# Output projection with MLP's first products: transposes half a tile later, another order of tile pairs, four of seven operands split in place

## The chip, the cores and the metric

The kernel runs on one core of a Trainium2 chip. The metric is the device time of one execution in microseconds, as the median over runs. Engines are named as in the profile: PE (TensorE; its weight loads are PEld), DVE (VectorE), ACT (ScalarE), POOL (GpSimd) and SP (SyncE, which here only issues DMAs). A DMA that POOL issues goes over its own queue.

## The reference, cut to what matters

One layer of an encoder over 2048 positions and 1024 channels. Attention and a Hyena operator each give 512 channels. The change touches what comes after them:

```
mix = concatenate([rms_norm(att, attn_out_g), rms_norm(hy, hy_out_g)], axis=-1)
h = h + mix @ w_out
m = rms_norm(h, norm2_g)
h = h + square(relu(m @ w_mlp_in)) @ w_mlp_out
return rms_norm(h, final_g)
```

All matrix products are made in three passes of a split format: an operand is written as high part + low part (a cast on ACT, then a subtraction on DVE), and high·high, high·low and low·high are added up in PSUM.

## The kernel before, in words

The positions lie in 16 tiles of 128. The output projection is made in two halves. The first, `att_part`, multiplies the attention channels; it is a generator that is advanced a step at a time (`pump(side)`) inside the long convolutions of `filter_dft` and `conv`, and writes `h` to `h_d`. A step is three matmuls; a tile has 8 steps.

The second half is `mix`. It runs 16 tiles in a hand-written order; on PE, DVE, ACT and POOL instructions stand in the order of the code, while SP's queue is ordered by the planner. For tile number `n` of the loop (its products are called P(n) here):

- `load` fetches `h` (3 buffers) and the two parts of the Hyena channels (3 sets of buffers), two tiles ahead, over SP.
- `products(u, j, ...)`: 2 column halves j of 4 x 3 matmuls each into a bank per half.
- `added(u, j)` (DVE, L843) takes the bank times the norm plus `h` into `h`. `squared` (ACT, L847) sums squares. `normed` (L855 to L864) writes `h` back to DRAM (the profile names this `h_d<-h`), works out the reciprocal root in five small DVE steps and one ACT square root, and writes `m`, half on DVE and half on ACT.
- `turned` (L870), called T(n) here, transposes `m` by 8 PE instructions into a bank pair. `taken` (L884) moves these with the gain by 8 ACT instructions into `sa` (first tile of a pair, 2 buffers) or `sb` (second tile; 1 buffer with places for 5 blocks: two for the tile itself, three for sums).

Two tiles of a pair (rows `i` and `i + 4` of a half, `half` 0 or 1) give seven operands of MLP's Strassen-Winograd product: four blocks of `m` and three sums of them, by four DVE subtractions (L894) that are queued in `sums` and called by `add_up`. `keep` (L891, POOL DMAs) copies each of the seven: for half 0 into the tiles `ml`, for half 1 into DRAM (`mo_d`). For half 0 a cast on ACT (L912, `cast`) writes `mh` from `ml`, and `rest` (L919, DVE) subtracts it to leave the low part in `ml`. In tile `n` of the loop before, P(n) comes first on PE and T(n-1) after it, once tile n-1 has been added, squared and normed.

Behind the last tile the generator `mlp_in` is advanced by `next(mlp)`: it casts MLP's weight operands (`prepare`, L1013 and L1014) and makes its first products g(block, p). Its first five products are written out in `mix`; the rest follow when `mix` is done. The sums of the weights for the second block (`left_sums`, L796 to L799) are POOL's.

Of the kernel before, what the change touches and what calls it, by code (L numbers as in the profile page):

```python
# [23 lines left out]
NT = SEQ // P  # L24
# [13 lines left out]
def f32(ap):  # L38
    return ap.bitcast(F32)
# [727 lines left out]
def att_part(k, pool, ps, ts):  # L767

    nc, x = k.nc, k.a["x"][0]
    ops = []  # L770
    yield from att_operands(k, ps, ts[0], ops)
    for i, t in enumerate(ts):
        nxt = []
        steps = att_operands(k, ps, ts[i + 1], nxt) if i + 1 < len(ts) else iter(())
        for j in range(2):
            at = slice(t * P, (t + 1) * P), slice(j * 512, (j + 1) * 512)
            h = pool.tile([P, 512], F32, name="h", bufs=HB)
            nc.sync.dma_start(out=h[:], in_=x[at])
            for _ in project(k, ps, j, h[:], k.wo0, *ops):
                pump(steps)  # L780
                yield
            nc.sync.dma_start(out=k.h_d[at], in_=h[:])
        ops = nxt
# [26 lines left out]
LAST_USED = 0, 1, 5, 2, 4, 3, 6  # L810


def mix(k, mo, pool, top, ps, wo, mlp):


    nc, a = k.nc, k.a
# [1 line left out]
    nc.scalar.dma_start(out=g2[:], in_=a["norm2_g"][0].rearrange("(d p) -> p d", p=P), allow_slow_non_contiguous=True)  # L818
    made = {(part, i): mo.tile([P, 4, 4, P], F32R, name=f"m{part}{i}", bufs=1) for i in LAST_USED for part in "hl"}
    k.mh, k.ml = ([made[part, i] for i in range(7)] for part in "hl")  # L820
    order = [(half, i, s) for half in range(2) for i in range(4) for s in range(2)]
    tiles = [8 * half + 4 * s + i for half, i, s in order]
    hr, = k.hr

# [26 lines left out]
        u.m = (pool if own else mo).tile([P, DM], F32, name="m", tag="h" if own else "raw", bufs=3 if own else NRAW)  # L851
        u.ssq = pool.tile([P, 1], F32, name="r2s", bufs=2)

    def normed(u):
        nc.sync.dma_start(out=k.h2_d[u.t * P:(u.t + 1) * P, :], in_=u.h[:])  # L855
        y, r, e = (pool.tile([P, 1], F32, name=f"r2{x}", bufs=2) for x in "yre")
        nc.vector.tensor_scalar(out=y[:], in0=u.ssq[:], scalar1=EPS, scalar2=None, op0=ALU.add)
        nc.scalar.activation(out=e[:], in_=y[:], func=AF.Sqrt)
        nc.vector.reciprocal(out=r[:], in_=e[:])
        nc.vector.tensor_mul(out=e[:], in0=r[:], in1=r[:])  # L860
        nc.vector.scalar_tensor_tensor(out=e[:], in0=e[:], scalar=-0.5, in1=y[:], op0=ALU.mult, op1=ALU.mult)
        nc.vector.scalar_tensor_tensor(out=r[:], in0=e[:], scalar=1.5, in1=r[:], op0=ALU.add, op1=ALU.mult)
        nc.vector.tensor_scalar_mul(out=u.m[:, :512], in0=u.h[:, :512], scalar1=r[:])
        nc.scalar.mul(out=u.m[:, 512:], in_=u.h[:, 512:], mul=r[:])  # L864
# [8 lines left out]
    def taken(u):  # L873


        half, i, s = u.order
        if s == 0:
            k.sa = pool.tile([P, 2, 4, P], F32, name="sa", bufs=2)
        else:
            k.sb = top.tile([P, 5, 4, P], F32, name="sb", bufs=1)  # L880
        b = k.sb if s else k.sa
        for c in range(2):
            for d in range(4):
                nc.scalar.mul(out=b[:, c, d], in_=u.tp[:, c, d * P:(d + 1) * P], mul=g2[:, 4 * c + d:4 * c + d + 1])  # L884
        if s:
            op = [k.sa[:, 0], k.sa[:, 1]] + [k.sb[:, j] for j in range(5)]
            b11, b21, b12, b22, t1, t2, t4 = op
            def keep(*js):
                for j in js:
                    dst = k.mo_d[j, :, i] if half else f32(k.ml[j][:, i])  # L890
                    nc.gpsimd.dma_start(out=dst, in_=op[j])  # L891

            def sub(out, in0, in1, *js):
                nc.vector.tensor_sub(out=out, in0=in0, in1=in1)  # L894
                keep(*js)

            keep(0, 1)
            sums.append(lambda: sub(t1, b12, b11, 4))
            sums.append(lambda: sub(t2, b22, t1, 5, 3))
            sums.append(lambda: sub(b12, b22, b12, 2))  # L900
            sums.append(lambda: sub(t4, b21, t2, 6))
            if not half:
                sums.append(lambda: splits.extend((j, i) for j in (0, 1, 5, 3, 4, 2, 6)))

    def add_up(n):
        for _ in range(min(n, len(sums))):
            sums.pop(0)()

    def cast(n):
        for _ in range(min(n, len(splits))):  # L910
            j, i = splits.pop(0)
            nc.scalar.copy(out=k.mh[j][:, i], in_=f32(k.ml[j][:, i]))  # L912
            casts.append((j, i))

    def rest():
        while casts:
            j, i = casts.pop(0)
            hi, lo = k.mh[j][:, i], k.ml[j][:, i]
            nc.vector.tensor_sub(out=lo, in0=f32(lo), in1=f32(hi))  # L919

    sums, splits, casts = [], [], []
    queue = [load(0), load(1)]
    old = older = None
    for n in range(NT):
        u = queue.pop(0)
        if n + 2 < NT:
            queue.append(load(n + 2))
        if n == NT - 2:
            next(mlp)
        if n == 0:  # L930
            v = queue[0]
            for w in (u, v):
                for j in range(2):
                    products(w, j, (0, 1, 2))
            for j in range(2):
                products(u, j, (3,))
        elif n == 1:
            for j in range(2):
                products(u, j, (3,))
        elif n < NT - 1:  # L940
            for j in range(2):
                products(u, j, range(4))
        else:
            for c in range(4):
                for j in range(2):
                    products(u, j, (c,))
        if old:
            added(old, 1)
            squared(old)
            rest()  # L950
            cast(1)
            normed(old)
            if older:
                taken(older)
            turned(old)
        room(u)
        if n < NT - 1:
            added(u, 0)
        if n % 2 == 0 or n == NT - 1:
            add_up(5)  # L960
        cast((2 - n % 2) if n < NT - 1 else 99)
        older, old = old, u
    rest()
    next(mlp)
    for j in range(2):
        added(old, j)
    next(mlp)
    squared(old)
    next(mlp)
    normed(old)  # L970
    next(mlp)
    taken(older)
    turned(old)
    next(mlp)
    taken(old)
    add_up(99)
# [2 lines left out]
LEAD = 5  # L979


def mlp_in(k, mo, ps):
# [78 lines left out]
    early = []  # L1061
    for x in seq[:2]:
        prepare(*x)
        early.append(product(*x))
    lefts(0)
    yield
    for x in seq[2:LEAD]:
        prepare(*x)
        if x is not seq[LEAD - 1]:
            yield  # L1070
    for x in seq[2:LEAD - 1]:
        early.append(product(*x))
    yield
    early.append(product(*seq[LEAD - 1]))
    yield
    held.update((name, tile(name, bufs)) for name, bufs in (("sn", 2), ("u2", 1), ("u4", 1), ("r", 4)))
    for i, (n, p) in enumerate(seq):
        if i + LEAD < len(seq):
# [562 lines left out]
def conv(k, o, c1, ps, side):  # L1641
# [104 lines left out]
    for gb in range(16):  # L1746
        cur = nxt
        if gb < 15:
            nxt = turned(gb + 1)
        if o and gb < 11:  # L1750
            pump(side, 10 ** 6 if gb == 10 else PUMP_C[3])
        both = c1.tile([P, 2, HYW], F32, name="both", tag="F", bufs=FB)
        gx, y = (both[:, i].rearrange("p (g m) -> p g m", m=P) for i in range(2))
        nc.sync.dma_start(out=gx, in_=gate[:, 4 * gb:4 * gb + 4])
        pair = ps.get("x", "yo")
        yo = pair[:, 0].rearrange("p (q g m) -> p q g m", q=2, m=HF)
        for q in range(2):
            for half in range(2):
                nc.tensor.matmul(yo[:, q], d4[:, q, half], cur[:, half, q], start=half == 0, stop=half == 1)  # L1759
        if squares:  # L1760
            ssq_add(pair[:, 1], *squares.pop(0))
        odd = c1.tile([P, 2, HYW], F32, name="odd", tag="t2", bufs=2)[:, 0, :4 * HF].rearrange("p (g m) -> p g m", m=HF)
        nc.scalar.copy(out=odd, in_=yo[:, 1])
        nc.vector.tensor_add(out=y[:, :, :HF], in0=yo[:, 0], in1=odd)
        nc.vector.tensor_sub(out=y[:, :, ::-1][:, :, :HF], in0=yo[:, 0], in1=odd)
        nc.gpsimd.tensor_mul(out=gx, in0=y, in1=gx)
        if o == 0:
            nc.sync.dma_start(out=dst[:, 4 * gb:4 * gb + 4], in_=gx)
            k.feed.limit += 1
            k.feed.fill(gb >= FOLD_C)  # L1770
            continue
        hl = cz.tile([P, 2, 4, P], F32R, name="zp", bufs=3)
        nc.gpsimd.tensor_copy(out=hl[:, 0], in_=gx)
        if made:
            parts(*made)
        made = gb, gx, y, hl
        if gb > 10:
            k.wo1 = next(weights, None) or k.wo1
    if not o:
        return  # L1780
    parts(*made)
    pair = ps.get("x", "yo")
    for i, x in enumerate(squares):
        ssq_add(pair[:, i], *x)
    k.hr = []
    pump(rstd_steps(k, k.wa, k.hssq[:], QW, NT, "hr", k.hr), 3)
    cz_pool.__exit__(None, None, None)
# [149 lines left out]
```

## Time and profile before

| | us |
|---|---|
| median of 3 runs | 3068.47 (3065.22 to 3071.64) |
| the profiled execution, its own time | 3065.21 |
| span of its profile | 3063.3 |
| PE busy in it | 2954.1 (96%) |
| stretch from P(2) to the end of P(14) | 1693.75 to 1788.72 |
| stretch from there to the third matmul of MLP's product g(1, 6) | 1788.72 to 1833.56 |

The profiled execution is 3.3 us below the median of the runs. Its span leaves out 1.9 us at the ends. Times of the rows below count from the start of the span.

### The profile page before, as it was taken

To read this page: it belongs to the slowest core of one execution; us is meant where nothing else is said; L and a number is where in the kernel's file an instruction comes from. 1 tells how busy PE (TensorE), PEld (TensorE's weight loads), DVE (VectorE), ACT (ScalarE), POOL (GpSimd) and SP (SyncE) were. 2 spreads that over 40 slices of the span, in tenths; PEclk is the share of its full clock that TensorE was granted. 3 is DMA by queue.
4 is the path that set the end of the run, shared out by engine and by line. 5 is a ranking of instruction groups with operands and counts; after the bars stand their busy time and mean duration, and the time that the engine had idled before them with its cause. 6 is when DMAs were issued, how large, how long until landed. Compare 5 with 4: busy or idle time off the path is not lost.

```text
span 3063.3 us, 40351 instructions
## 1 busy us (share of the span) xinstructions
PE 2954.1 (96%) x13386; PEld 2231.2 (73%) x13386; DVE 2071.5 (68%) x3141; ACT 1389.7 (45%) x2593; POOL 1661.3 (54%) x1393
## 2 busy tenths in 40 slices
PE   7997999999999999999999889999999899999998
PEld 6785666666666666765858768887888688888887
DVE  6777877777777766667474568778877544454455
ACT  6765555555555555552534653334333233223333
POOL 4356887878778780025555129777877452250010
PEclk9999999999999999999999999999999999999999
DMA  9766433252343247785747875446544493433454
GB/s 255 221 180 210 150 117 109 95 162 100 112 146 107 95 129 220 252 282 166 220 133 208 297 256 170 152 151 218 171 152 152 167 332 111 141 107 132 154 183 150
DMA packets 452049, 525.75 MB, mean 172 GB/s; under 512 B 30442, under 2 KB 315616, under 8 KB 444800
## 3 DMA queue, kind: packets, MB, share of 16 engines
q1 hardware_dynamic: 440064, 490.65, 49.3%
q0 software_dynamic: 7728, 28.02, 2.6%
q10 hardware_dynamic: 4048, 4.49, 0.5%
q8 instruction: 107, 1.75, 0.2%
q14 instruction: 102, 0.84, 0.1%
HBM read 321.72 MB, written 193.99 MB: 168 GB/s over the span
## 4 chain that ended last, share of the span: by engine, by line
PE 51%; DMA 3%; issue 3%; POOL 2%; ACT 1%; DVE 1%; SPq 0%; POOLq 0%; ACTq 0%; DVEq 0%
PE y L160 7%; PE y L161 7%; PE y L162 7%; PE g L162 6%; PE g L161 6%; PE g L160 5%; PE X L1553 4%; PE b L1692 2%; PE fs L1579 2%; PE yo L1759 2%; PE op L162 1%; PE op L160 1%; PE op L161 1%; DMA ml<-sb 1%; PE bt L1718 1%
## 5 line engine op out<-in xcount | busy, mean ns | idle before, releaser
L589 POOL TENSOR_TENSOR sum<-sum,p 128x512 f32<-128x512 f32 x403 | 537.0, 1333 | 98.7 <-ACT p L584 73.6
L564 DVE TENSOR_REDUCE top<-sc 128x1 f32<-128x512 f32 x512 | 344.6, 685 | 172.2 <-PE sc L561 169.3
L584 ACT ACTIVATE p<-st 128x512 f32<-128x512 f32 x512 | 302.3, 597 | 295.6 <-PE st L582 277.8
L160 PE MATMUL g<-mh,wop 128*128 128x512 f32 x896 | 351.4, 392 | 5.8 <-ACT wop L1013 5.8
L161 PE MATMUL g<-ml,wop 128*128 128x512 f32 x896 | 351.2, 392 | 4.0 <-DVE ml L1024 4.0
L162 PE MATMUL g<-mh,wop 128*128 128x512 f32 x896 | 350.8, 392 | 1.9 <-DVE wop L1014 1.9
L160 PE MATMUL y<-bh,ah 128*128 128x512 f32 x768 | 300.0, 391 | 11.1 <-ACT ah L1218 11.1
L1197 DVE TENSOR_TENSOR ah<-ar,ah 128x1024 fp32r<-128x1024 f32 x111 | 150.0, 1352 | 229.9 <-ACT ah L1196 226.8
L161 PE MATMUL y<-bh,ah 128*128 128x512 f32 x768 | 299.8, 390 | 0.0
L162 PE MATMUL y<-bh,ah 128*128 128x512 f32 x768 | 299.7, 390 | 0.0
L1196 ACT CAST ah<-ar 128x1024 fp32r<-128x1024 f32 x111 | 116.7, 1052 | 342.5 <-PE y L162 335.5
L602 PE MATMUL o<-p,vt 128*64 128x512 f32 x1024 | 236.6, 599 | 0.0
L561 PE MATMUL sc<-kt,q 128*128 128x512 f32 x512 | 203.6, 401 | 11.0 <-DVE top L564 5.2
L581 PE MATMUL st<-q,kt 128*128 128x512 f32 x512 | 213.0, 416 | 0.7 <-ACT p L584 0.5
L582 PE MATMUL st<-q,kt 128*128 128x512 f32 x512 | 201.5, 394 | 0.0
L160 PEld LDWEIGHTS g<-mh,wop 128*128 128x128 f32 x896 | 169.5, 189 | 41.8 <-ACT wop L1013 6.5
L161 PEld LDWEIGHTS g<-ml,wop 128*128 128x128 f32 x896 | 169.5, 189 | 40.3 <-DVE ml L1024 5.0
L162 PEld LDWEIGHTS g<-mh,wop 128*128 128x128 f32 x896 | 169.6, 189 | 38.5 <-DVE wop L1014 3.1
L1013 ACT CAST wop<-ws 128x512 fp32r<-128x512 f32 x128 | 79.3, 621 | 226.7 <-PE g L162 179.2
L160 PEld LDWEIGHTS y<-bh,ah 128*128 128x128 f32 x768 | 144.8, 189 | 42.1 <-ACT ah L1218 11.5
L162 PEld LDWEIGHTS y<-bh,ah 128*128 128x128 f32 x768 | 144.7, 188 | 30.3 <-DVE ah L1219 0.3
L161 PEld LDWEIGHTS y<-bh,ah 128*128 128x128 f32 x768 | 144.7, 188 | 29.9
(338 smaller groups left out, 6956.1 us busy)
## 6 DMA issues: line engine op xcount, KB each, us to landing
ar<-H_d SPq DMA_DIRECT2D x109, 512.0 KB, 3.8
uw<-uw_d SPq DMA_DIRECT2D x36, 1024.0 KB, 4.9
w1raw<-in_w_mlp_in SPq DMA_DIRECT2D x64, 512.0 KB, 4.1
H_d<-r SPq DMA_DIRECT2D x96, 256.0 KB, 2.2
H_d<-s SPq DMA_DIRECT2D x96, 256.0 KB, 2.0
F_d<-F SPq DMA_DIRECT2D x34, 512.0 KB, 3.4
F<-F_d SPq DMA_DIRECT2D x34, 512.0 KB, 3.7
taps_d<-both SPq DMA_DIRECT2D x64, 256.0 KB, 2.0
```

The source lines that it names most:

```text
L160: mm(out, l_hi, r_hi, start=start, stop=False)
L161: mm(out, l_hi, r_lo, start=False, stop=False)
L162: return mm(out, l_lo, r_hi, start=False, stop=stop)
L561: nc.tensor.matmul(s[:], u.q[:, h], kt[u.kv, b][0][:], start=True, stop=True)
L564: nc.vector.tensor_reduce(out=u.top[:, h, b:b + 1], in_=s[:], axis=AX.X, op=ALU.max, negate=True)
L581: nc.tensor.matmul(s[:], lo[:, c], u.q2[:].rearrange("p h t -> p (h t)"), start=True, stop=False)
L582: nc.tensor.matmul(s[:], hi[:, c], u.q[:].rearrange("p h t -> p (h t)"), start=False, stop=True)
L584: nc.scalar.activation(out=p[:], in_=s[:], func=AF.Exp)
L589: u.adder.tensor_add(out=u.sum[:], in0=u.p0[:] if j == 1 else u.sum[:], in1=p[:])
L602: nc.tensor.matmul(u.o[cols], vt[j // 8][:, j % 8, u.kv], p[:], start=j < 2, stop=j > 13)
L1197: nc.vector.tensor_sub(out=h[:, 1], in0=raw[:], in1=f32(h[:, 0]))
L1553: k.nc.tensor.matmul(d[:, ri], t[:, m], Af[:, 2 * j + at], start=True, stop=True)
```

## The change: what it does

1. T(n-2) now stands between the two column halves of P(n), where before T(n-1) stood behind P(n). In the last tile, number 15, T(13) stands in its middle; T(14) and T(15) stand among MLP's first products.
2. The pairs are taken in the order `PAIRS` (half, row): a pair of half 1 comes third, and the last three are of half 1. Before, all of half 0 came first.
3. In half 0, `keep` copies only the operands 2, 3 and 6 (`GATHERED`) to `ml`. The other four (0, 1, 4, 5) are cast from where they stand in `sa` and `sb`, and the subtraction writes the low part to `ml`. Half 1 still copies all seven.
4. The four subtractions of a pair are called singly or two at a time in two tiles. Casts come one behind the squares, one behind the square root and, from tile 9 on, one more. `taken` comes last in a tile. All casts are done in tile 14.
5. `mlp_in` yields more often, and its first cast (the weights of g(0,1)) is issued in tile 15, before that tile's norm; the rest are spread over the tail in another order.
6. `att_part` counts how many tiles it has left (`k.att_left`). Where `conv` before pumped it to its end at block 10, it now stops there with two tiles left, and pumps these at the end of `conv`.

```
+        k.att_left = len(ts) - i
...
+PAIRS = (0, 0), (0, 1), (1, 0), (0, 2), (0, 3), (1, 1), (1, 2), (1, 3)
+GATHERED = 2, 3, 6
...
-    order = [(half, i, s) for half in range(2) for i in range(4) for s in range(2)]
+    order = [(half, i, s) for half, i in PAIRS for s in range(2)]
...
-    def normed(u):
+    def normed(u, between):
...
         nc.scalar.activation(out=e[:], in_=y[:], func=AF.Sqrt)
+        for f in between:
+            f()
...
+                    if half:
+                        nc.gpsimd.dma_start(out=k.mo_d[j, :, i], in_=op[j])
+                    elif j in GATHERED:
+                        nc.gpsimd.dma_start(out=f32(k.ml[j][:, i]), in_=op[j])
...
+                if not half:
+                    splits[:0] = [(j, i, op[j]) for j in js if j not in GATHERED]
...
-                sums.append(lambda: splits.extend((j, i) for j in (0, 1, 5, 3, 4, 2, 6)))
+                n0 = next((x for x, y in enumerate(splits) if y[2] is None), len(splits))
+                splits[n0:n0] = [(j, i, op[j]) for j in (0, 1)]
+                sums.append(lambda: splits.extend((j, i, None) for j in GATHERED))
...
-            nc.scalar.copy(out=k.mh[j][:, i], in_=f32(k.ml[j][:, i]))
-            casts.append((j, i))
+            src = f32(k.ml[j][:, i]) if src is None else src
+            nc.scalar.copy(out=k.mh[j][:, i], in_=src)
+            casts.append((j, i, src))
...
-            for j in range(2):
-                products(u, j, range(4))
+            products(u, 0, range(4))
+            turned(older)
+            products(u, 1, range(4))
         else:
             for c in range(4):
                 for j in range(2):
                     products(u, j, (c,))
+                if c == 1:
+                    turned(older)
         if old:
             added(old, 1)
             squared(old)
+            add_up(1)
+            cast()
+            if n == NT - 1:
+                next(mlp)
+            normed(old, (rest, cast))
+            if n > 8:
+                cast()
             rest()
-            cast(1)
-            normed(old)
-            if older:
-                taken(older)
-            turned(old)
         room(u)
         if n < NT - 1:
             added(u, 0)
-        if n % 2 == 0 or n == NT - 1:
-            add_up(5)
-        cast((2 - n % 2) if n < NT - 1 else 99)
+        if older:
+            taken(older)
+        add_up(2 if n < NT - 2 else 99)
+        if n == NT - 2:
+            cast(99)
+            rest()
...
+    next(mlp)
+    older, old = us[-2:]
+    next(mlp)
+    turned(older)
     next(mlp)
     for j in range(2):
         added(old, j)
-    next(mlp)
     squared(old)
     next(mlp)
-    normed(old)
     next(mlp)
+    normed(old, ())
     taken(older)
+    next(mlp)
+    next(mlp)
     turned(old)
+    next(mlp)
+    next(mlp)
+    add_up(99)
     next(mlp)
     taken(old)
...
-            pump(side, 10 ** 6 if gb == 10 else PUMP_C[3])
+            pump(side, PUMP_C[3])
+            while gb == 10 and k.att_left > 2:
+                pump(side)
...
+    pump(side, 5)
     pair = ps.get("x", "yo")
     for i, x in enumerate(squares):
         ssq_add(pair[:, i], *x)
+        pump(side, 10 ** 6 if i else 4)
```

## Rows read from the trace of the kernel before

**Rows 1.** Stretches: busy us of each engine, granted clock, DMA share, GB/s.

```profile
1693.75:1788.72 94.97, 86.72 (x411) 70.20 (x409) 59.02 (x141) 62.36 (x169) 19.76 (x37) 0.96 0.88 303
1788.72:1833.56 44.84, 34.21 (x148) 26.69 (x147) 28.36 (x56) 22.55 (x61) 15.28 (x23) 0.92 0.63 210
1833.56:2090.00 256.44, 256.44 (x1124) 212.24 (x1125) 205.26 (x226) 83.53 (x140) 195.72 (x139) 0.99 0.48 158
```

**Rows 2.** What PE waited for, 1693.75 to 1833.6: us, times, longest.

```profile
PE mt L870 <- DVE m L863: 11.1, 9, 3.0
PE g L160 <- ACT wop L1013: 5.8, 2, 4.5
PE g L162 <- DVE wop L1014: 1.9, 2, 1.4
```

**Rows 3.** PE in order of time: start, us, instruction, idle before it and releaser.

```profile
1614.82 0.39 PE L162 MATMUL op<-wo,ol 128*128 128x512 f32 x1
...
1690.97 0.49 PE L162 MATMUL op<-wo,ol 128*128 128x512 f32 x1
1692.93 1.07 PE L870 MATMUL mt<-ident,m 128*128 128x128 f32 x8 [1.47 <-DVE m L863]
...
1705.77 1.03 PE L870 MATMUL mt<-ident,m 128*128 128x128 f32 x8
...
1712.21 1.03 PE L870 MATMUL mt<-ident,m 128*128 128x128 f32 x8
...
1743.13 1.94 PE L870 MATMUL mt<-ident,m 128*128 128x128 f32 x8 [2.95 <-DVE m L863]
...
1803.95 0.80 PE L160 MATMUL g<-mh,wop 128*128 128x512 f32 x1 [4.51 <-ACT wop L1013]
...
1833.56 0.51 PE L162 MATMUL g<-mh,wop 128*128 128x512 f32 x1 [0.52 <-DVE wop L1014]
```

**Rows 4.** The chain that ended last, one lap of a pair: start, us, what.

```profile
1720.60 2.17 ACT sb L884 x8
...
1737.34 2.17 ACT sb L884 x8
...
1740.03 1.05 ACT m L847 x2
...
1744.28 1.90 DVE sb L894 x3
...
1746.85 6.76 DMA ml<-sb
1753.69 2.17 ACT sb L884 x8
```

**Rows 5.** ACT in order of time: norms of tiles 1 and 6, and a late `sb`.

```profile
1696.58 0.72 ACT L864 ACTIVATE m<-h,r2r 128x512 f32<-128x512 f32 x1 [0.87 <-DVE r2r L862]
...
1730.12 1.06 ACT L847 ACTIVATE m<-h 128x1024 f32<-128x1024 f32 x1 [0.50 <-DVE h L843]
...
1731.18 0.61 ACT L912 CAST mh<-ml 128x512 fp32r<-128x512 f32 x1
...
1733.07 0.72 ACT L864 ACTIVATE m<-h,r2r 128x512 f32<-128x512 f32 x1 [0.88 <-DVE r2r L862]
...
1801.22 2.17 ACT L884 ACTIVATE sb<-mt,g 128x128 f32<-128x128 f32 x8 [2.69 <-DMA mo_d<-sb]
```

**Rows 6.** DVE's additions (`added`), 1690 to 1834: busy us, mean ns, idle before.

```profile
L843 DVE SCALAR_TENSOR_TENSOR h<-op,hr,h 128x512 f32<-128x512 f32 x30 | 21.9, 746 | 5.6 <-PE op L162 5.6
```

**Rows 7.** The copies by POOL out of `sb`: their issues, and issue to landing.

```profile
L891 POOL DMA_DIRECT2D ml<-sb x20: 537/537/539, 1711.6 to 1763.2; - x20
...
DMA to landing us min/median/max: 2.5/4.1/7.1
```

**Rows 8.** SP's queue, 1690 to 1834: what it waited for, us, times, longest.

```profile
SPq L829 <- DMA h_d<-h: 43.9, 11, 6.6
```

**Rows 9.** The writes of `h` (L855), issue to landing.

```profile
DMA to landing us min/median/max: 3.4/5.7/9.3
```

More of the change, by code (lines that the diff above doesn't have):

```diff
@@ L889, in keep @@
                 for j in js:
-                    dst = k.mo_d[j, :, i] if half else f32(k.ml[j][:, i])
-                    nc.gpsimd.dma_start(out=dst, in_=op[j])
+                    if half:
+                        nc.gpsimd.dma_start(out=k.mo_d[j, :, i], in_=op[j])
+                    elif j in GATHERED:
+                        nc.gpsimd.dma_start(out=f32(k.ml[j][:, i]), in_=op[j])
             def sub(out, in0, in1, *js):
@@ L907, in add_up, with cast @@
             sums.pop(0)()
-    def cast(n):
+    def cast(n=1):
         for _ in range(min(n, len(splits))):
-            j, i = splits.pop(0)
-            nc.scalar.copy(out=k.mh[j][:, i], in_=f32(k.ml[j][:, i]))
-            casts.append((j, i))
+            j, i, src = splits.pop(0)
+            src = f32(k.ml[j][:, i]) if src is None else src
+            nc.scalar.copy(out=k.mh[j][:, i], in_=src)
+            casts.append((j, i, src))
     def rest():
         while casts:
-            j, i = casts.pop(0)
-            hi, lo = k.mh[j][:, i], k.ml[j][:, i]
-            nc.vector.tensor_sub(out=lo, in0=f32(lo), in1=f32(hi))
+            j, i, src = casts.pop(0)
+            nc.vector.tensor_sub(out=k.ml[j][:, i], in0=src, in1=f32(k.mh[j][:, i]))
     sums, splits, casts = [], [], []
-    queue = [load(0), load(1)]
-    old = older = None
+    us, queue = [], [load(0), load(1)]
     for n in range(NT):
         u = queue.pop(0)
+        us.append(u)
+        old, older = (us[n - i] if n >= i else None for i in (1, 2))
         if n + 2 < NT:
@@ L930, in mix @@
         if n == 0:
-            v = queue[0]
-            for w in (u, v):
+            for w in (u, queue[0]):
                 for j in range(2):
@@ L958, in mix @@
             added(u, 0)
-        if n % 2 == 0 or n == NT - 1:
-            add_up(5)
-        cast((2 - n % 2) if n < NT - 1 else 99)
-        older, old = old, u
+        if older:
[4 more added lines that the diff above has]
+            rest()
     rest()
+    next(mlp)
+    older, old = us[-2:]
+    next(mlp)
+    turned(older)
     next(mlp)
@@ L1063, in mlp_in @@
         prepare(*x)
+        yield
+    for x in seq[:2]:
         early.append(product(*x))
+        yield
     lefts(0)
     yield
-    for x in seq[2:LEAD]:
+    prepare(*seq[2])
+    yield
+    early.append(product(*seq[2]))
+    yield
+    for x in seq[3:LEAD]:
         prepare(*x)
-        if x is not seq[LEAD - 1]:
-            yield
-    for x in seq[2:LEAD - 1]:
+        yield
+    for x in seq[3:LEAD]:
         early.append(product(*x))
-    yield
-    early.append(product(*seq[LEAD - 1]))
-    yield
+        yield
     held.update((name, tile(name, bufs)) for name, bufs in (("sn", 2), ("u2", 1), ("u4", 1), ("r", 4)))
```

## The prediction

> **What bounds the kernel now.** I read the page's engine table first, then the busy time of the stretches around the change, then PE's waits, then PE in order of time, then the chain that ended last, then ACT, DVE and the DMAs. Behind the output projection PE is busy without a gap (the third stretch, 256.44 of 256.44 us) [rows 1], so whatever PE gains before g(1,6) moves the end of the kernel by as much. The question is only how early PE reaches g(1,6). Two stretches before it have idle PE: 8.3 of 95 us in the loop and 10.6 of 45 us behind it [rows 1]. Both also run in part below full clock, at a mean of 0.96 and 0.92.
>
> Without a wait the loop takes 1712.21 − 1705.77 = 6.44 us a tile, 24 products and 8 transposes [rows 3]: a matmul goes out about every 0.23 us. PE's waits are of two kinds [rows 2]: the transposes wait for `m` (11.1 us in nine waits), and MLP's first products wait for their cast weights (7.7 us in four). The wait for `m` is not DVE being slow. The chain shows the lap: ACT moves a tile into `sb` (1737.34), squares the next (1740.03), DVE makes the sums (1744.28), POOL copies them (1746.85), and only when the copy has landed may ACT write `sb` again (1753.69 is the next) [rows 4]. A lap is 16.1 us a pair on average ((1801.22 − 1720.60) / 5 [rows 4, 5]), and PE needs 2 x 6.44 = 12.88. While ACT stands before `sb`, the next tile's square and norm stand behind it in ACT's queue; so `m` is late, PE waits, and after the longest wait PE falls to its lower clock level: eight transposes took 1.94 us at 1743.13 where they took 1.03 at 1712.21 [rows 3].
>
> **The change part by part.**
>
> *The attention piece (item 6): nothing.* `att_part` has 5 + 16 x 8 = 133 steps. Counted in the code, it is pumped 8 times at the end of the first filter stage, 6 + 16 x 2 = 38 in each of two filters and 4 + 16 + 2 x 3 = 26 in each of two convolutions: 8 + 76 + 52 = 136. It is used up before the blocks at which the new stop stands. The trace agrees: its last product is at 1614.82 [rows 3]. So the stop finds one tile left by its count and the new pumps find an empty generator. If a few steps were left, two tiles of 24 matmuls at 0.23 (11 us) would move; they would fill waits or move PE's work, so at most a few us either way.
>
> *The first transposes: 2.3 us gained.* T(0) held PE from the end of P(1), 1690.97 + 0.43 = 1691.4, to the start of P(2) at 1693.75. Now P(2) starts at once. Its operands must have landed; if not, the gain is nothing.
>
> *The loop: PE's need.* P(2) to P(15) with one transpose block each: 14 x 6.44 = 90.2 us, so at best P(15) ends at 1691.4 + 90.2 = 1781.6.
>
> *The loop: ACT's lap.* A tile's norm, from the start of its square to the end of `m`, took 1733.07 + 0.63 − 1730.12 = 3.6 us, a cast already in between [rows 5]. The new order puts one subtraction (0.6; three sums of this size took 1.90 [rows 4]) on DVE between root and reciprocal: 4.2. Then `taken`, 2.05: 6.2 us a tile, and from tile 9 on a third cast of 0.5 before `taken`: 6.7. Behind the second tile of a pair two sums must end before DVE adds the next tile: 0.65 past the move, then 0.75 for the addition [rows 6] and a hop of 0.05: 1.45. A pair costs ACT 2 x 6.2 + 1.45 = 13.85, later 14.9, against PE's 12.88. ACT loses 1.0 a pair, then 2.0.
>
> *The loop: `sb`'s lap.* Half 0 copies 3 blocks instead of 7, and the last one (operand 6) now waits for the last sum, which comes behind the norm and the next addition: square 1.45 past the move, 3.2 to DVE's half of `m`, 0.4 for that, 0.6 for a subtraction, 0.65 for the addition, 0.65 for the sum itself: 7.0 (later 0.9 more with the third cast and its subtraction). Then POOL's 0.54 and the landing of one copy. I take the median, 4.1, between 2.5 and 7.1 [rows 7]. With the move of 2.17 the lap is 13.8, later 14.7: the same as ACT's own. With 2.5 it is hidden; with 7.1 it is 16.8 to 17.7, the lap of before and more. The Trainium skill (DMA: Bandwidth & Descriptors, Anatomy of one DMA — SWDGE (gpsimd) path) states a fixed part of about 2.0 us and bytes over 436 GB/s, which I work out to 2.6 us for a block of 256 KB; the median in the trace is 1.5 longer, under load. By the page alone the tail below would come out some 1.5 us earlier.
>
> *What the later transpose gives.* `m` of tile 2 is ready at about 1702.3 (tile 1's norm is done at 1696.58 + 0.63 = 1697.2 [rows 5], ACT then does `taken(0)`, 2.0, and a norm with no cast yet takes 3.6 − 0.5 = 3.1). PE wants it at 1691.4 + 2 x 6.44 + 2.8 = 1707.1: 4.8 us ahead. By ACT's lap this lead shrinks by 1.0 a pair to 1.8 at tile 8, then by 2.0 a pair to −2.2 at tile 12, and by another 1.7 (the half of a pair that has the sums) to −3.9 at tile 13. So PE waits about 3.9 us in all, spread over T(10) to T(13), where it waited 11.1 and lost some 4 to the clock. P(15) ends at 1781.6 + 3.9 = 1785.5.
>
> *The tail.* From P(15)'s end to g(1,6) PE has eight products of 12 matmuls (2.73 each) and T(14), T(15): 23.4. The waits, ACT and DVE laid in order from ACT's lap: weights of g(0,1) are cast behind the square of tile 14, 0.7 + 0.2 late. Those of g(0,2) stand on ACT behind `taken(13)`, which waits for the copy of the sum before it (1788.7 to 1790.8), and their low part on DVE behind all four sums: 1.6 + 1.1. g(0,6) waits for DVE's weight sums, 0.9 + 0.9; g(0,7) stands behind `taken(14)`, 1.5 + 0.2. Together 7.1. So g(1,6) may start at 1785.5 + 23.4 + 7.1 = 1816.0. POOL's weight sums for it wait for the copies out of `sb`, as before; T(15) now stands two products further from g(1,6), so these are ready at about 1815. Before, g(1,6) stood as if started at 1833.56 − 2 x 0.23 = 1833.1 [rows 3]. The difference is 17.1 us.
>
> *What is charged against it.* SP's queue: a load of `h` waits for the write of an earlier tile to land, 11 times, up to 6.6 us [rows 8], and the next write stands behind that load. A landing of 5.7 [rows 9] and some 1.2 of issues make 6.9 a tile, more than 6.44; over 14 tiles 6.5 us late, of which the loads' lead hides some 4. I charge 1.5 (0 to 4). The clock: one more drop in the tail costs about 15 matmuls at 0.43 instead of 0.23, 3 us, as after the wait of 4.51 [rows 3]; at even odds 1.5 (0 to 3). Data is no bound: at 303 GB/s with a share of 0.88 [rows 1] full use is 344 GB/s, and the loop moves 11 copies fewer (2.9 MB of 28.8), 75 us of transfer in 84.
>
> Sum: 17.1 − 1.5 − 1.5 = 14.1 us. From the profiled execution, 3065.2, that gives 3051.1; the median of the runs stands 3.3 above it, so 3054.
>
> **The rivals.**
>
> - *Every wait goes* (chance 0.07). If ACT's lap keeps to 12.88, all of 1833.1 − 1691.4 − 90.2 − 23.4 = 28.1 us is gained: 3040. For it: ACT is busy only 62 of 95 us [rows 1]. Against: its lap is made of hops, not of work.
> - *The gain is lost in the tail* (0.15). Three of the four waits there each bring the low clock: 3 x 3.3 = 10 us. 17.1 − 1.5 − 10 = 5.6: 3063. For it: the wait of 4.51 did so. Against: the new waits are 1 to 3 us, and one of 1.47 was followed by transposes at full rate [rows 3].
> - *SP's queue sets the pace* (0.13). If the loop goes on at 94.97 / 13 = 7.3 us a tile because `h` comes late, only the first transposes (2.3) and the tail's 7 are gained: 3059. For it: the landing of 9.3 [rows 9]. Against: the loads' lead.
> - *Slower, by the last copy's landing* (0.05). Operand 6 is now copied alone and last, behind a 512 KB write of `h`. Each us of landing above 7.1 adds 6 us over six laps; at 7.1 the loop's loss eats the other 9.4 us of gain; above 8.1 the kernel is slower by over 0.2%. At 9.3, the longest landing of a write, it is 3081. Against: 7.1 is the longest of all copies out of `sb` [rows 7], which went five in a row. The Trainium skill (SBUF — State Buffer, SBUF: two separate sides) says that a DMA issued by POOL can stand for want of descriptors while DVE runs certain copies, some 2.5 us longer; by it the landing would be 6.6 and the time about 3063. The trace shows no sign of it at the issue, 537 to 539 ns in twenty of them [rows 7].
>
> **How the numbers follow.** The forecast has 0.60, with its own range 3050 (no charge, a landing of 2.5) to 3059 (both charges in full). 0.2%, about what a measurement of this kernel can tell from no change, is 6 us: faster is below 3062.3. The forecast, the first rival and most of the third are faster: 0.77. The second and the rest of the third: same, 0.18. The last: 0.05. The range reaches to 3045 and 3064.
>
> **What would show it.** T(n) without waits up to tile 9 and about 4 us of them by tile 13; laps of `sb` of 14 to 15 us; P(2) at about 1691.5; attention's products ending at 1614.8 as before; g(0,2) and g(0,7) waiting for ACT's casts. Wrong would make it: a lap of 16, waits of DVE's addition for `h`, or PE at the low clock in the tail.

## The result, and the profile after

The changed kernel takes 3055.48 us (median of 8 runs, 3044.51 to 3058.98) against 3071.05 (median of 8, 3065.22 to 3072.96) run beside it: a ratio of 0.9944, interval 0.9933 to 0.9955, about 17 us faster (15.6 by the medians). The forecast was 3054.

The profiled execution of the changed kernel (3044.51) is 11.0 us under its median, that of the kernel before (3065.21) 5.8, so two traces side by side overstate the gain. I therefore set each trace against one instant just ahead of the change: the last group of selection matmuls (`yo<-sel`), 1680.28 before and 1679.74 after. The ninth of MLP's first products, g(1,6), starts at 1833.1 before [rows 3] and 1816.59 after: 16.5 us earlier, 0.54 of it already there, so **16.0 us from the change**: 13.4 up to the last matmul of P(15) (it starts 117.1 us behind that instant before and 103.6 after), the rest behind it. Of the kernel before:

```profile
1680.28 1.03 PE L1742 MATMUL yo<-sel,both 128*128 128x16 f32 x8 [0.33 <-DVE hssq L1743]
...
1797.36 0.40 PE L162 MATMUL op<-wo,ol 128*128 128x512 f32 x1
...
1834.65 0.63 PE L160 MATMUL g<-mh,wop 128*128 128x512 f32 x1
```

What follows g(1,6) took 3063.3 − 1833.1 = 1230.2 before and 3042.7 − 1816.6 = 1226.1 after. Some 1.7 of these 4.1 are the change's too: behind the late start of g(1,6), eight matmuls of the kernel before ran at a lower granted clock (1834.65 is the first), and the twelve from 1833.56 took until 1838.01, 4.45 us, where twelve at full clock take 2.73. The changed kernel starts g(1,6) without a wait and shows none of this. With them the traces give the change 17.7 us. What the other 2.4 are stays open.

Stretches of the changed kernel, one line each: from the first transposes to the end of the last tile's products, and from there to g(1,6) (columns as in [rows 1]):

```profile
core 0: us, PE busy (x) PEld busy (x) DVE busy (x) ACT busy (x) POOL busy (x), PEclk, DMA share, GB/s
1693.74:1783.60 89.86, 87.64 (x437) 72.07 (x435) 66.56 (x156) 67.16 (x185) 14.29 (x27) 1.00 0.90 300
1783.60:1817.00 33.40, 27.73 (x115) 20.96 (x115) 22.68 (x42) 18.62 (x49) 12.46 (x18) 0.95 0.64 210
```

The loop is full: 2.2 us of idle PE where there were 8.3 [rows 1], at full granted clock, and POOL's copies are down to 27 instructions. The DMA share is still 0.90. The tail keeps 5.7 us of idle PE and a clock of 0.95. PE's waits, 1685 to 1835:

```profile
PE g L160 <- ACT wop L1043: 3.2, 3, 1.2
PE op L162 <- DMA ol<-zp_d: 2.7, 1, 2.7
PE g L162 <- DVE wop L1044: 2.4, 2, 1.3
PE mt L878 <- DVE m L871: 2.2, 3, 1.3
```

Set against [rows 2], the waits for `m` fell from 11.1 to 2.2 (the 2.7 for `ol` stand ahead of the first transposes, in both kernels: 3.0 before). PE in order of time:

```profile
1614.22 0.39 PE L162 MATMUL op<-wo,ol 128*128 128x512 f32 x1
...
1679.74 1.04 PE L1776 MATMUL yo<-sel,both 128*128 128x16 f32 x8 [0.34 <-DVE hssq L1777]
...
1690.80 0.47 PE L160 MATMUL op<-wo,mx 128*128 128x512 f32 x1
...
1693.74 1.04 PE L878 MATMUL mt<-ident,m 128*128 128x128 f32 x8
...
1764.93 1.06 PE L878 MATMUL mt<-ident,m 128*128 128x128 f32 x8 [0.41 <-DVE m L871]
...
1771.98 1.06 PE L878 MATMUL mt<-ident,m 128*128 128x128 f32 x8 [0.49 <-DVE m L871]
...
1779.93 1.06 PE L878 MATMUL mt<-ident,m 128*128 128x128 f32 x8 [1.32 <-DVE m L871]
...
1783.38 0.39 PE L162 MATMUL op<-wo,ol 128*128 128x512 f32 x1
1784.98 0.50 PE L160 MATMUL g<-mh,wop 128*128 128x512 f32 x1 [1.21 <-ACT wop L1043]
...
1790.17 0.50 PE L160 MATMUL g<-mh,wop 128*128 128x512 f32 x1 [1.03 <-ACT wop L1043]
...
1792.20 0.50 PE L162 MATMUL g<-mh,wop 128*128 128x512 f32 x1 [1.29 <-DVE wop L1044]
...
1795.37 0.63 PE L161 MATMUL g<-ml,wop 128*128 128x512 f32 x1
...
1801.11 0.50 PE L160 MATMUL g<-mh,wop 128*128 128x512 f32 x1 [0.99 <-ACT wop L1043]
...
1807.21 0.39 PE L161 MATMUL g<-ml,wop 128*128 128x512 f32 x1
1808.74 0.50 PE L162 MATMUL g<-mh,wop 128*128 128x512 f32 x1 [1.14 <-DVE wop L1044]
1809.07 0.39 PE L160 MATMUL g<-mh,wop 128*128 128x512 f32 x1
...
1816.59 0.39 PE L160 MATMUL g<-mh,wop 128*128 128x512 f32 x1
```

Attention's last product is where it was (1614.22 against 1614.82 [rows 3]). P(2) starts at 1690.80, ahead of any transposes. T(0) to T(10) wait for nothing, T(11) to T(13) for 2.2 us. The tail has five short waits, and behind the wait at 1792.20 eight matmuls at a lower granted clock: 1795.37 is one, 0.63 long and 0.43 from the next, where one at full clock is 0.39 long and 0.23 from the next. ACT's moves into `sb`:

```profile
1701.58 2.16 ACT L892 ACTIVATE sb<-mt,g 128x128 f32<-128x128 f32 x8
...
1715.05 2.16 ACT L892 ACTIVATE sb<-mt,g 128x128 f32<-128x128 f32 x8
...
1728.53 2.16 ACT L892 ACTIVATE sb<-mt,g 128x128 f32<-128x128 f32 x8
...
1742.70 2.18 ACT L892 ACTIVATE sb<-mt,g 128x128 f32<-128x128 f32 x8
```

None has a wait for a copy (one of before's stands in [rows 5]). Laps: 13.47, 13.48, 14.17 in these rows and 14.93, 14.99, 14.83 in the next, where before made 16.1. SP's queue still waits for the writes of `h` (1690 to 1800), but less than in [rows 8]:

```profile
SPq L835 <- DMA h_d<-h: 37.4, 10, 5.8
```

### The profile page after: what moved, and what is told of

Same layout as the page of the kernel before. It is cut to its first block, busy times and chain, and to the rows that moved or that the text cites. A ratio compares the mean times of both kernels' runs of the same rounds, so it can differ in the third digit from the quotient of the medians.

```text
span 3042.7 us, 40324 instructions
## 1 busy us (share of the span) xinstructions
PE 2948.4 (97%) x13386; PEld 2227.8 (73%) x13386; DVE 2070.8 (68%) x3141; ACT 1390.4 (46%) x2593; POOL 1653.3 (54%) x1377
## 4 chain that ended last, share of the span: by engine, by line
PE 51%; issue 4%; POOL 3%; ACT 1%; DMA 1%; DVE 1%; SPq 0%; POOLq 0%; ACTq 0%; DVEq 0%
PE y L160 7%; PE y L161 7%; PE y L162 7%; PE g L162 5%; PE g L161 5%; PE g L160 5%; PE X L1587 4%; PE b L1726 2%; PE yo L1795 2%; PE fs L1613 2%; PE cs L1693 1%; PE op L162 1%; PE op L160 1%; PE op L161 1%; PE bt L1752 1%
## 5 line engine op out<-in xcount | busy, mean ns | idle before, releaser
L1230 ACT CAST ah<-ar 128x1024 fp32r<-128x1024 f32 x111 | 117.1, 1055 | 344.4 <-PE y L162 333.2
```

## The experiments

The times of all experiments, each in 5 to 11 runs beside the kernel before on the same chip, as ratios to it. An interval is 3 to 4 us to either side, so differences under some 5 us between two rows are not told apart by these alone; the traces resolve more, each of one execution. "To g(1,6)" is the time from the selection matmuls to the start of g(1,6) in the one profiled execution (where its third matmul waits, 0.46 ahead of that, as in [rows 3]); what the clock does behind g(1,6) is not in it.

| kernel | ratio (interval) | us from before | to g(1,6) |
|---|---|---|---|
| before | 1 | 0 | 152.8 |
| changed | 0.9944 (0.9933 to 0.9955) | −17 | 136.9 |
| changed, all seven copied | 0.9963 (0.9951 to 0.9976) | −11 | 145.1 |
| changed, sixteen idle transfers more | 0.9957 (0.9943 to 0.9970) | −13 | 146.2 |
| changed, transposes half a tile earlier | 0.9960 (0.9946 to 0.9973) | −12 | 140.7 |
| changed, pairs in the old order | 0.9945 (0.9933 to 0.9958) | −17 | 137.8 |
| changed, first cast late | 0.9939 (0.9926 to 0.9951) | −19 | 139.8 |
| before, late transposes alone | 0.9985 (0.9976 to 0.9994) | −5 | 153.6 |
| before, split in place alone | 0.9983 (0.9974 to 0.9992) | −5 | 153.2 |
| before, `sb` in three tiles | 0.9986 (0.9977 to 0.9995) | −4 | 156.9 |
| changed, `sb` in three tiles | 0.9932 (0.9920 to 0.9944) | −21 | 137.5 |
| changed, root first | 0.9943 (0.9931 to 0.9954) | −18 | 136.9 |
| changed, both of these | 0.9933 (0.9921 to 0.9945) | −21 | 135.5 |
| both of these and another tail | 0.9926 (0.9913 to 0.9938) | −23 | 135.5 |

### All seven copied again

```
-GATHERED = 2, 3, 6
+GATHERED = 0, 1, 5, 3, 4, 2, 6
...
-                splits[n0:n0] = [(j, i, op[j]) for j in (0, 1)]
+                splits[n0:n0] = [(j, i, op[j]) for j in (0, 1) if j not in GATHERED]
```

> The change with one part undone: in half 0 all seven operands are copied out of sb and sa again and cast from the copies, instead of four split in place; order of pairs, late transposes and the order on ACT stay. Theory (the loop's pace is the lap of sb: move, sums, the copy issued last, its landing): the copy of operand 6 now stands on the same queue as before behind four more copies of a half-0 pair, so sb's lap grows by what the landing is late; with the landing of the profiled execution before (4.1 median) nothing, with 7.1 about 3 us a pair on five pairs of half 0, less the slack. I expect 2 to 8 us slower than the changed kernel, and waits of sb's write for a copy back on ACT. Rival (it is the norm no longer standing behind the write of sb, and the later transposes, that brought the gain; splitting in place matters nothing): within 1 us of the changed kernel, laps of sb still 13.5 to 15.

By the ratios 6 us of the gain are lost (0.9963 against 0.9944, with intervals that just overlap), by the traces to g(1,6) 8. The laps of `sb` are 14.2 to 16.7 with waits for copies, as the theory had it. But PE waits for `m` no longer than without the copies. What it waits for is new, the low parts of its own operands. PE's and SP's waits, from 1698 (columns as above):

```profile
PE op L162 <- DMA ol<-zp_d: 3.2, 4, 1.1
...
PE mt L878 <- DVE m L871: 2.0, 2, 1.3
PE op L162 <- DMA mx<-zp_d: 1.7, 2, 1.1
...
SPq L835 <- DMA h_d<-h: 53.2, 12, 7.8
```

And the whole loop has more on its DMA engines (share 0.93, 324 GB/s):

```profile
1700.37:1796.70 96.33, 89.39 (x437) 71.48 (x435) 65.40 (x154) 66.72 (x184) 22.79 (x43) 1.00 0.93 324
```

So the price may be `sb`, held longer, or the load. The next run adds load without holding `sb`.

### Sixteen transfers that nothing waits for

```
+                    else:
+                        w = f32(wo[0][0][:, :512]).rearrange("p (a b) -> p a b", b=P)
+                        nc.gpsimd.dma_start(out=k.x_d[(0, 1, 4, 5).index(j), :, i], in_=w)
```

> The changed kernel with sixteen transfers more: wherever a pair of half 0 no longer copies an operand, POOL issues a copy of equal size (256 KB) of a constant weight block to scratch memory. Nothing in the kernel waits for these, and sb is not held by them; the output is the same. The run with all operands copied lost 6 us, with PE waiting for its operand loads 4.9 us and laps of sb of 14.2 to 16.7. Theory A (that loss is load: more bytes make the writes of h land later, SP's queue stands before the next load of h, and the low operand parts queued behind it come late): the same loss, 4 to 7 us against the changed kernel, with waits of PE for operand loads of over 3 us, while ACT waits little before sb. Theory B (that loss is sb held longer, by the copies of its blocks): within 2 us of the changed kernel.

Theory A: to g(1,6) it takes 146.2, even more than with the real copies (145.1); by the medians 4.8 us are lost against the changed kernel, by the ratios 4.0, with intervals that overlap. PE waits 6.4 us for low operand parts and never for `m`. Its waits from 1698, and SP's queue around the longest:

```profile
PE op L162 <- DMA ol<-zp_d: 3.2, 2, 1.8
PE op L162 <- DMA mx<-zp_d: 3.2, 1, 3.2
...
SPq L835 <- DMA h_d<-h: 58.7, 11, 8.4
```

```profile
1749.44 0.42 SPq L861 DMA_DIRECT2D h_d<-h  x1
1749.96 0.45 SPq L752 DMA_DIRECT2D mx<-zp_d  x1
1758.92 0.32 SPq L835 DMA_DIRECT2D h<-h_d  x1
1759.33 0.38 SPq L752 DMA_DIRECT2D mx<-zp_d  x1
```

```profile
1764.99 0.80 PE L162 MATMUL op<-wo,mx 128*128 128x512 f32 x1 [3.17 <-DMA mx<-zp_d]
```

One lap of SP's queue is: write of `h`, high part, load of `h`, low part. The load stands until the write has landed (1749.44 to 1758.92), the low part goes out behind it (1759.33), and PE's third matmul stands for it until 1764.99. Among these three kernels the write lands sooner the less is in flight: the median is 6.0 us in the changed kernel, 6.5 with all seven copied, 6.9 here. So load alone is enough to cost about what the copies cost, and in the loop of both runs PE stands for operands and hardly for `m`. That `sb`'s longer laps would cost nothing is not shown: here too ACT waits 4.6 us for copies out of `sb` (4.2 with all seven copied), and a PE that stands for operands asks for `m` later. Nor are the two loads alike: the idle transfers write to DRAM and landed in 7.2 us (median), the copies into `ml` in 5.0.

### Transposes half a tile earlier

```
-            products(u, 0, range(4))
             turned(older)
+            products(u, 0, range(4))
             products(u, 1, range(4))
```

(and in the last tile likewise)

> The change with the transposes of a tile placed half a tile earlier: before the next tile's products instead of between their halves. Theory (the lead of m over the transposes shrinks by ACT's lap against PE's need, and was at its end 2.2 us short in the changed kernel): every transpose block asks 12 matmuls earlier, 2.8 us, so the lead is used up some tiles earlier and PE waits 2.8 us more in the loop, in all about 5 us; the kernel is about 3 us slower than the changed one, if no wait brings the low clock, 6 if one does. Rival (the half tile is the change's main gain): the waits of the kernel before come back, over 9 us in the loop, 10 us slower. Second rival (nothing hangs on it): within 1 us.

By the ratios 5 us of the gain are lost (the intervals overlap), by the traces to g(1,6) 3.8. The waits for `m` are 7.8 us in eight, 1.5 of them at T(0); none is over 1.7 and the loop keeps the full clock. The waits lie between theory (5) and rival (over 9), the time is nearer to the theory's.

### The old order of pairs, and the first cast late

```
-PAIRS = (0, 0), (0, 1), (1, 0), (0, 2), (0, 3), (1, 1), (1, 2), (1, 3)
+PAIRS = (0, 0), (0, 1), (0, 2), (0, 3), (1, 0), (1, 1), (1, 2), (1, 3)
```

> The change with the pairs of tiles in their old order: all four pairs of half 0, then the four of half 1. Theory (a pair costs ACT 13.9 or 14.9 by whether its third cast runs in it, and PE is bound by neither order): the same number of casts, copies and sums in other tiles, within 2 us of the changed kernel. Rival (the order spreads the casts and gathers, so that half 1's seven copies and the casts do not fall together at the end): more than 3 us slower, the T waits of the last pairs growing.

```
-            if n == NT - 1:
-                next(mlp)
             normed(old, (rest, cast))
...
     rest()
     next(mlp)
+    next(mlp)
```

> The change with the cast of the first MLP weights (for g(0,1)) issued after the loop, as in the kernel before, instead of ahead of tile 14's norm. Theory (g(0,1) waits on ACT behind tile 14's norm, and the tail's waits are in a row, so what one waits the next need not wait in full): g(0,1) waits about 3 to 5 us instead of 1.2, a part is regained at g(0,2) and g(0,7); 2 to 5 us slower in all. Rival (the tail is bound by the last of ACT's and POOL's chain to g(1,6), whatever is cast first): within 1 us.

Neither costs anything by the clock. The order of pairs leaves the waits of the loop as they are, 2.2 us in three. With the late cast the trace shows why it is free:

```profile
PE g L160 <- ACT wop L1042: 5.3, 1, 5.3
...
PE g L162 <- DVE wop L1043: 0.8, 1, 0.8
```

g(0,1) waits 5.3 instead of 1.2, and no later product for its high part at all. From the last of P(15) to g(1,6) it is 33.4 us, with the early cast 33.2: one long wait has the place of five short ones. (The 2.9 by which the trace is longer to g(1,6) arise almost all in the loop, ahead of that.) The rival holds in the time, but not by its reason: g(1,6), whose chain it named, waits for nothing in either trace.

### The kernel before with one part alone

Late transposes alone: `turned(older)` between the halves of `products`, `turned(old)` behind `taken` left out, T(14) behind the loop.

> The kernel before with one part of the change alone: the transposes of a tile stand half a tile later on PE, between the two halves of the next tile's products. Order of pairs, copies, casts and the order on ACT stay as before. Theory (the part is worth a fixed lead: the first transposes no longer hold PE, 2.3 us, and PE asks for m 12 matmuls later, 2.8 us, while ACT's lap of 16 us a pair stays and eats the rest): 4 to 6 us faster than the kernel before, waits for m and laps near 16 us still there. Rival 1 (the late transposes are most of the change): more than 10 us faster, waits for m under 4 us. Rival 2 (a later transpose makes ACT's lap later by the same amount, since its move waits for it): within 1 us of before.

Split in place alone: as in the change, with (4, 5, 0, 1) put at the front of the casts when the last sum is made.

> The kernel before with another part of the change alone: in half 0 operands 0, 1, 4 and 5 are split in place, from sa and sb, ahead of the copied ones in the list of casts, and only 2, 3 and 6 are copied out. Order of pairs, transposes, and the places of casts and sums stay. Theory (before's loop had two bounds at once, sb's lap with its copies and the load on the DMA engines; the late transposes alone lift neither, and four copies fewer lift both): sb's lap falls by the four issues of 0.54 us and by a shorter landing, from 16.1 to about 14 us a pair in half 0, waits for m from 11 to 4 to 7 us; 4 to 8 us faster than the kernel before, PE without waits for operand loads. Rival (the parts work only together: without the late transposes PE still stands for m as long): within 2 us of before.

Each gains about 5 us by the times, as the theories said, though not in the way. With late transposes the waits for `m` do fall (2.1), but PE now waits 6.9 for operand parts, and what the loop gains (its end comes 3.7 earlier against the selection matmuls) is lost again at the first product of MLP, whose cast is no earlier:

```profile
1807.98 0.79 PE L160 MATMUL g<-mh,wop 128*128 128x512 f32 x1 [7.98 <-ACT wop L1016]
```

Where it was 4.51 [rows 3]. With splitting in place the profiled execution took 3075.92 us where the median is 3069.06, so its trace does not show the gain. In it PE waits for no operand in the loop and SP for only 28.0 us, and some laps of `sb` are short (13.1, 13.5), but they are 16.0 on average, as before: copies out of `sb` land up to 9.6 us after their issue, ACT stands for 5.5 and 6.0 us, and PE waits 4.8 and 5.0 for `m`, each followed by a lower granted clock. ACT's moves, and the first of these waits on PE:

```profile
1764.61 2.18 ACT L884 ACTIVATE sb<-mt,g 128x128 f32<-128x128 f32 x8 [5.52 <-DMA ml<-sb]
...
1796.92 2.19 ACT L884 ACTIVATE sb<-mt,g 128x128 f32<-128x128 f32 x8 [6.04 <-DMA mo_d<-sb]
```

```profile
1770.39 1.94 PE L870 MATMUL mt<-ident,m 128*128 128x128 f32 x8 [4.81 <-DVE m L863]
```

The two parts come near to adding up: alone they gain 4.6 and 5.2 us, taken out of the changed kernel they cost 4.9 and 5.8, each known to 3 to 5 us. By these figures some 7 us of the 17 belong to neither. Order of pairs and first cast are not it. What is left are the sums spread over the pair, DVE's addition ahead of the move, and the new order behind the loop; I did not part these.

### `sb` in three tiles, root first, and both

```
-            k.sb = top.tile([P, 5, 4, P], F32, name="sb", bufs=1)
+            k.sb = top.tile([P, 2, 4, P], F32, name="sb", bufs=1)
+            k.st = top.tile([P, 2, 4, P], F32, name="st", bufs=1)
+            k.s4 = top.tile([P, 4, P], F32, name="s4", bufs=1)
...
-            normed(old, (rest, cast))
+            normed(old, (cast,))
```

> The kernel before with sb cut into three tiles of the same memory in all: the two blocks that ACT moves, the two sums of t1 and t2, and the sum t4. ACT's write then waits only for the copies of its own two blocks (operands 2 and 3), not for the copy of t4, which is issued last. Theory (the pace of the loop before, 16.1 us a pair, is the lap from ACT's write over the sums and the last copy back to ACT's write): the copy of operand 6 and its landing no longer bound the write, the lap shortens by one or two copies' issue, 0.5 to 1 us, and the wait for sb on ACT falls; 3 to 6 us faster than the kernel before. Rival (the pace is ACT's own order of work, the wait for sb only stands where other waits would stand): within 1 us of before.

> The changed kernel with sb cut into three tiles of the same memory in all. Theory (in the changed kernel ACT no longer waits for a copy before it writes sb, so the laps of 13.5 to 15 are ACT's own row of work): nothing to gain, within 1 us of the changed kernel, laps of sb equal. Rival (the copy of operand 6, which is issued last and alone, still sets the lap): laps shorter by 0.5 to 1 us, the 2.2 us of waits for m gone, 2 to 4 us faster.

> The changed kernel without the subtraction between root and reciprocal: DVE makes the low part of a split after the norm instead of inside it, so m comes about 0.5 us earlier in each tile. Theory (ACT's lap bounds the pace, the copy of operand 6 stands just under it): the lap of a pair falls by up to 1 us until the copy's landing bounds it (13.8 and 14.7 by the prediction's sum); waits for m fall from 2.2 to about 1; 0.5 to 2 us faster, and ACT may wait for copies before sb. Rival (the subtraction lies under ACT's cast, so it costs nothing): within 0.5 us, laps as they were.

> Both at once: sb in three tiles and no subtraction between root and reciprocal. Theory: with the copy no longer able to bound the lap, ACT's lap falls by up to 1 us a pair to about 13 and 14, the waits for m (2.2 us) vanish and the tail's waits get shorter by about as much; 3 to 5 us faster than the changed kernel. Rival (PE's end is set in the tail by casts that stand behind the last norms): within 1 us of the root-first kernel.

In the kernel before the three tiles gain 4 us by the clock, but not in the trace (laps of 15.7 to 17.7; ACT still waits 17.9 us for the copies of the two blocks themselves); the profiled execution took 3071.36 where the median is 3067.03, and what the 4 us are stays open. In the changed kernel they leave the laps at 13.5 to 15.9, so those were ACT's; the 3.7 us that the ratios show are not in the trace either, whose execution took 6 us more than the median, and the intervals overlap. Root first alone brings laps of 13.1 to 15.1, and ACT then waits for copies:

```profile
ACT sb L892 <- DMA ml<-sb: 1.9, 3, 0.8
```

So the copies stand just under ACT's lap. With both, the laps are 13.08, 13.25, 13.76, 14.45, 14.45, 14.85, ACT waits for no copy and PE never for `m`. By the ratios that is 3.4 us under the changed kernel, with intervals that overlap; the trace is 1.4 us shorter to g(1,6), not 3 to 5, since the tail keeps its 33.2: at full granted clock now (1.00), but with 6.8 us of waits where there were 5.7.

### Another tail

On top of both: MLP's first two weight blocks cast ahead of tile 14's square and of tile 13's move; tile 15 added and squared ahead of the sums of tile 13's pair, which now stand behind two more casts.

```
             added(old, 1)
+            if n == NT - 1:
+                next(mlp)
             squared(old)
...
+        if n == NT - 1:
+            next(mlp)
         if older:
             taken(older)
-        add_up(2 if n < NT - 2 else 99)
+        add_up(99 if n == NT - 2 else 2 if n < NT - 2 else 0)
...
     rest()
-    next(mlp)
...
     normed(old, ())
-    taken(older)
     next(mlp)
     next(mlp)
+    add_up(99)
+    taken(older)
+    next(mlp)
     turned(old)
...
-    add_up(99)
-    next(mlp)
     taken(old)
```

> The kernel with sb in three tiles and no subtraction between root and reciprocal, and the tail in another order: the first two MLP weight blocks are cast ahead of tile 14's square and ahead of tile 13's move; tile 15 is added and squared before the sums of tile 13's pair; two more weight blocks are cast before tile 14's move, and the sums of tile 13's pair stand behind them. Theory (the tail's waits for casts and weight sums, 5.7 us, and its stretch of low clock come from ACT's and DVE's order, not from their work): the stretch from the last product of the output projection to the 97th of MLP's first products shrinks from 33.2 to 27 to 30 us, bounded by POOL's weight sums for g(1,6), which still stand behind the last pair's copies; 3 to 6 us faster than the changed kernel by this part and 3 by the rest. Rival (POOL's sums are as late as before or later, or another cast takes the place): stretch 32 us or more, no faster than without the reordering.

The fastest of all: 0.9926, 3049.8 us, about 5.5 us under the changed kernel, with intervals that overlap a little. But from the last of P(15) to g(1,6) it is 31.9 us, where the theory had 27 to 30 and the rival 32 or more; beside the same kernel without the reordering (33.2, and 0.9933) 1.3 us are shown, not more. PE now waits for ACT's moves (2.2 and 1.0), and g(1,6) itself for its own cast, which follows POOL's sums, the bound that the theory named:

```profile
PE g L160 <- ACT sb L894: 2.2, 1, 2.2
```

```profile
1818.25 0.50 PE L160 MATMUL g<-mh,wop 128*128 128x512 f32 x1 [0.60 <-ACT wop L1046]
```

## Why the prediction was right, step by step

- **The attention piece: nothing.** Right. Its last product ends as far ahead of the selection matmuls as before (65.5 us).
- **First transposes, 2.3 us.** Right: P(2) starts at 1690.80, 2.4 us earlier when the 0.54 are taken off.
- **ACT's lap, 13.85 and later 14.9.** Right: 13.5 to 14.2, then 14.8 to 15.0. The run with three tiles shows that these laps are ACT's own.
- **`sb`'s lap, 13.8 and 14.7, hidden.** Right, and as close as worked out: take half a microsecond a tile from ACT, and it waits for copies. The landing is the median that the sum took, or a little longer: 4.6 between 2.5 and 8.3. The 2.6 us worked out from the Trainium skill (DMA: Bandwidth & Descriptors, Anatomy of one DMA — SWDGE (gpsimd) path) was the lower edge. The 6.6 us by the Trainium skill (SBUF — State Buffer, SBUF: two separate sides) did not come about as a typical value, and POOL's issues stay at 0.54. But what four copies fewer bring was put down to this lap alone; the run with idle transfers shows that a like load costs about as much without holding `sb`.
- **Waits for `m`, 3.9 us over T(10) to T(13).** 2.2 over T(11) to T(13): right in kind and place, 1.7 too high.
- **The tail, waits of 7.1.** Five waits, 5.7 in all, four of them those foreseen. That of g(0,6) did not come, and the third matmul of g(1,1) waited 1.1 unforeseen. Yet the tail took 33.0 (1783.6 to 1816.6) and not 30.5. The lower clock cost 1.5, which the charge of 1.5 had. The other term that was mis-sized is the price of a wait: around 1808.74 PE loses 1809.07 − 1807.21 − 2 x 0.23 = 1.40 where the profile lists 1.14, since it counts from the end of the matmul before, 0.16 past its slot, and the first pitch behind is 0.33. Five waits make some 1.4 us. Of the 1.0 that is left, half are two waits too short for the list: the matmuls at 1785.70 and 1801.84 stood 0.15 and 0.16 past their slots, at 0.26 lost each.
- **The charge for SP's queue, 1.5.** None in this trace. In five traces whose loop differs little (old order, late cast, three tiles, root first, both) PE waited 0 to 2.3 us for low operand parts, 1.2 on average.
- **"Data is no bound."** This is the step that was wrong, though it cost the forecast little. A mean rate below the full one does not show that a transfer is in time. The DMA share of the loop stays at 0.90, and sixteen transfers of 256 KB, which nobody reads, take back 4 to 5 us of the gain. The rival on SP's queue named the right wait and the wrong victim: not the load of `h` comes late, but the low operand part that stands behind it in the queue.
- **The tail's rival** may have been nearer than its 0.15: with the late transposes alone the gain of the loop is lost at g(0,1) (7.98). Whether the re-ordered tail or ACT's shorter lap keeps that from happening in the changed kernel is not shown; the early first cast is not what does it.
- **"Whatever PE gains before g(1,6) moves the end by as much."** Not quite: a stretch in which PE is busy without a gap can still hold matmuls at the lower clock. The 1.7 us behind g(1,6) were in no term of the sum.

Sum: the prediction had 17.1 less 3.0 of charges, 14.1; the trace has 16.0, with the clock behind g(1,6) 17.7, the runs 15.6 to 17. Up to g(1,6) the loop came out 1.4 better and SP's charge of 1.5 was not needed, while the tail was 1.0 longer than forecast with its charge. The forecast also stood on a median of three runs before (3068.47), which is 3071.05 in eight. That 3054 lies 1.5 from the measured 3055.48 is in part luck: the gain was 1.5 to 3 us more than forecast, and the time that it was taken from was 2.6 higher.

## What to carry to other kernels

When one wait is taken away, list what the next transfers wait for in their own queue: an in-order DMA queue in which a load waits for a write's landing holds every load behind it, and adding transfers that nobody waits for is a quick test of how near that is. Two bounds that stand close together (here an engine's lap and a buffer's lap) give little when only one is lifted; undo each part and also try each alone. In a row of short waits, an edit that ends the first of them may only lengthen the next.

## What the runs showed of the hardware

The unforeseen wait at 1808.74 is DVE's. A subtraction there took 1.97 us, with a sum by POOL beside it; with none beside it the same operation took 0.68 to 0.69. DVE, then POOL, of the changed kernel:

```profile
1806.71 1.97 DVE L1044 TENSOR_TENSOR wop<-ws,wop 128x512 fp32r<-128x512 f32 x1
```

```profile
1806.84 1.29 POOL L797 TENSOR_TENSOR ws<-w1raw 128x512 f32<-128x512 f32 x1
```

1.97 − 0.68 = 1.29 is just POOL's sum. In the run with three tiles and root first it was the same, 1.98 with a sum of 1.29 beside it; in the run with another tail, where these casts go before POOL's sums, the subtraction took 0.68, and this wait does not occur (g(1,1) waits for ACT's move instead). The Trainium skill (SBUF — State Buffer, SBUF: two separate sides) says that DVE and POOL share one pair of ports, which one holds for a whole instruction while the other stands; these rows agree. Which of the two took them first the start times do not tell: DVE, which stood, is listed 0.13 ahead.

A copy of 256 KB out of `sb` landed between 2.2 and 9.6 us after its issue in the run with splitting in place alone, the median being 4.2; the two that PE's longest waits go back to decide more there than the median does.
